# A seventh k-tile pair in Strassen's form, at the second piece, in seven units of a decoder trunk

## The chip, the core and the metric

The kernel runs on one core of one Trainium2 chip. Its time is device microseconds of one execution; the time before is the median of three runs. The profile is of one further execution. Engines: PE is TensorE (PEld its weight loads), DVE VectorE, ACT ScalarE, POOL GpSimd, SP SyncE, which issues most loads.

## The reference

One layer of a decoder trunk, for 256 rows of width 4096, all in fp32:

```python
u = rmsnorm(h, norm_w)
proj = u @ w_in            # a_q a_f a_i a_g  b_q b_k b_v b_g  gate_a gate_b
o_a = rmsnorm(hgrn2_mix(a_q, a_f, a_i, lb), hgrn_norm_w) * silu(a_g)
o_b = rmsnorm(diff_attention(b_q, b_k, b_v, lam, slopes), subln_w) * (1 - lam_init) * silu(b_g)
y = sigmoid(gate_a) * (o_a @ w_branch_a) + sigmoid(gate_b) * (o_b @ w_branch_b)
out = rmsnorm(h + y @ w_out, final_w)
```

`w_in` is 4096 x 24576, the two branch matrices are 2048 x 4096, `w_out` is 4096 x 4096. HGRN2 is a gated recurrence in chunks of 64 rows (16 heads); the differential attention has 8 heads of two maps.

## The kernel before

**Split numbers.** Each fp32 operand is held as two parts of the type fp32r, a high part (a copy of the number) and a low part (the number minus the high part). A product of two 128-deep tiles is three matmuls: high with high, high with low, low with high (L285 to L287, `mm`). For the weights the high part is made by ScalarE (L164, `hi`) and the low part by VectorE (L165, `lo`).

**Units and pieces.** The work is a list of units, each a matrix product that gives 256 rows by 1024 columns. A unit takes its weights in pieces of 128 x 2048 (1 MB): one piece is a pair of k-tiles (256 deep) by 1024 columns. There are 16 mixer units (0 to 7 for the four HGRN groups, two each; 8 to 15 for the four attention groups, two each) and 8 gate units (0 to 7), each of 16 pieces; 8 branch units of 8 pieces; 4 output units of 16 pieces. In a group the first unit gives the channel rows (forget and q, or q and k), the second the gate and the values.

**Plain and Strassen pieces.** A plain piece (kind P) is 8 products of 128 x 128 by 128 x 512, that is 24 matmuls, into the banks 0 to 3 of PSUM. A piece of kind S is done in the Winograd variant of Strassen's form: 7 products, 21 matmuls, into the banks P1, p5, P6, P7, 0, 1 and 2. For it the sums of the left operand (`s_form`, L376) are made once per k-tile pair and kept in the pool `sp` or `sp2` for all units that use them; the sums of the weights are made for each piece by VectorE, in place (L156, L142, L144). The order of the products in an S piece is, by chunk: 0 and 1; p5 and P1; P6; P7 and 2 (L264, `ORDER`). The four banks P1 to P7 are combined when the unit's last S piece is done (L305 to L323). `SPLIT` (L439) says which pieces of mixer units 3 to 15 and of gates 0 and 1 are S: six, from piece 3 on. `SPLIT_G` (nine, piece 1 among them) holds for gates 2 to 6. Mixer units 0 to 2 and gate 7 are plain; while unit 1 runs, u is normalised, and while unit 2 runs, the sums of u are made (`u_sums`, L455). The sums that only `SPLIT_G` needs are made in gate 1 (`more_sums`, L462), into `sp2`.

**Chunks and rings.** The parts of a piece are made in chunks: two of 1024 columns for a plain piece; three of 1024 and one of 512 for an S piece (its third). They go through a ring of six slots for `hi` and six for `lo`, five chunks ahead of use (L146, L171), so a chunk can be made when the one six before it has been used. The last pair of a unit keeps both of its chunks to the unit's end, since its products are done bank by bank. Raw weights have three buffers of 1 MB, filled by SyncE's queue.

**The order of work.** The framework orders each engine's instructions itself, by priority among those that are ready by its own estimate of time; the split of the weights runs under a raised priority (`AHEAD`, L40, L151). So the order in a queue may differ from that of the program.

**What runs beside the units.** The elementwise and small matrix work of the groups stands in a list (`todo`, L217), whose items are TensorE items (transposes, scores, outputs: they borrow one of the four banks P1 to P7 through `spare`, L61, in the order P6, P7, P1, p5) or plain ones. After each piece `step` (L222) takes from its head: a plain item, after which it returns, or up to two TensorE items, these only after the pieces in `OPEN` (L232), when the S products do not use the four banks. For an HGRN group the items run as follows: the first unit's four results are transposed (two after its last piece, two after piece 0 of the second unit; L752, L780), then `s1b`, `s1c`, `s1d`, `s2` (L796 to L826) come one per piece, then the three scores (L828) after pieces 14 and 15, then the two output products (`pv`, L845), one after piece 15 and one after piece 0 of the next unit, then the closing steps (`finish`, L688: root, sigmoid gate L699, scaling L706), and the transposes of the result (L709) after piece 14.

Of the kernel before, what the change touches and what calls it, by code (L numbers as in the profile page):

```python
# [19 lines left out]
S = 256  # L20
# [23 lines left out]
def trunk_kernel(ctx, tc, xT, x, nw, w_mix, w_gate, w_branch, w_out, lbt, hnw, lamv, slw, fw, out):  # L44
# [5 lines left out]
    wraw = ctx.enter_context(tc.tile_pool(name="wraw", bufs=3))  # L50
    whi = ctx.enter_context(tc.tile_pool(name="whi", bufs=6))
    wlo = ctx.enter_context(tc.tile_pool(name="wlo", bufs=6))
    sp = ctx.enter_context(tc.tile_pool(name="sp", bufs=6))
    gp = ctx.enter_context(tc.tile_pool(name="gp", bufs=5))
    psb = ctx.enter_context(tc.tile_pool(name="psb", bufs=1, space=PSUM))
    dram = ctx.enter_context(tc.tile_pool(name="dram", bufs=1, space=DRAM))
# [4 lines left out]
    def spare(shape, name):  # L61

        spare.at += 1
        return psb.tile(shape, F32, name=name, tag=f"b{(6, 7, 4, 5)[spare.at % 4]}")
# [152 lines left out]
    todo = deque()  # L217

    def later(f, pe_=False):
        todo.append((f, pe_))  # L220

    def step(n):  # L222
        for _ in range(2):
            if not todo or (todo[0][1] and n not in OPEN):
                return
            f, pe_ = todo.popleft()
            if f is not None:
                f()
            if not pe_:
                return  # L230

    OPEN = (14, 15, 0, 1, 2)  # L232


    plan = []

    def add(srcs, fn, kinds, post=None):

        for n, s in enumerate(srcs):
            stream.append(s, kinds[n])  # L240
            plan.append((n, fn, post))

    def run(upto):
        for i in range(run.at, upto):
            n, fn, post = plan[i]
            stream.load_to(i + LOAD_AHEAD)
            for c, (hi, lo) in enumerate(stream.take(i)):
                fn(n, c, hi, lo)
            if post:
                post(n)  # L250
            step(n)
        run.at = upto

    run.at = 0
# [14 lines left out]
    def wide_unit(srcs, kinds, pf, sf, bank, final, post=None, tail=1, kt0=0, pre=None):  # L269
# [62 lines left out]
        def fn(n, c, hi, lo):  # L332
# [19 lines left out]
            for blocks in ([[(t, 1 - m)] for t in range(2) for m in range(2)] if tail == 1  # L352
                           else [[(0, 0), (0, 1)], [(1, 0)], [(1, 1)]]):
                for (k, c2), w in held.items():
                    plain(k, c2, *w, blocks)

        add(srcs, fn, kinds, post)

    PLAIN = ["P"] * 16

    def mix(n, s):
        return ["S" if i in s else "P" for i in range(n)]

    def gate_unit(q, kinds, sf, bank, post=None):
        def final(t, n, ps, g):
            if g is None:
                g = gp.tile([P, 512], F32, name="gt", tag="gt")
                act.activation(g, ps, AF.Sigmoid)
            else:
                dve.tensor_tensor(g, ps, g, op=ALU.add)  # L370
                act.activation(g, g, AF.Sigmoid)
            pool.dma_start(g_dram[2 * q + n][t], g)

        wide_unit([w_gate[q, n] for n in range(16)], kinds, u, sf, bank, final, post)

    def s_form(f):  # L376

        s = gp.tile([P, 4, P], F32, name="s", tag="gt")
        a11, a21, a12, a22 = (f[:, k, t * P : (t + 1) * P] for k in range(2) for t in range(2))
        dve.tensor_tensor(s[:, 0], a21, a22, op=ALU.add)  # L380
        dve.tensor_tensor(s[:, 1], s[:, 0], a11, op=ALU.subtract)
        dve.tensor_tensor(s[:, 2], a21, a11, op=ALU.subtract)
        dve.tensor_tensor(s[:, 3], a12, s[:, 1], op=ALU.subtract)
        t = s_pool().tile([P, 4, 2, P], F32R, name="sf", tag="sf")
        act.activation(t[:, :, 0, :], s, AF.Copy)
        dve.tensor_tensor(t[:, :, 1, :], s, f32(t[:, :, 0, :]), op=ALU.subtract)
        return t
# [5 lines left out]
    def joined(n):  # L393

        f = gp.tile([P, 2, S], F32, name="f", tag="gt")
        t, k = u[n // 2], 2 * (n % 2)
        dve.tensor_tensor(f, f32(t[:, k : k + 2, 0, :]), f32(t[:, k : k + 2, 1, :]), op=ALU.add)
        return f
# [37 lines left out]

    SPLIT = (3, 5, 7, 9, 11, 13)  # L439
    SPLIT_G = (1, 3, 5, 6, 7, 9, 11, 13, 14)  # L440
    us = {}
    s_pools = [sp]
# [12 lines left out]
    def u_sums(which):  # L455
        def f(n):
            if n in which:
                us[n] = s_form(joined(n))
        return f


    def more_sums(n):  # L462
        if n == 0:
            s_pools[:] = [sp2]
        if n in SPLIT_G and n not in SPLIT:
            us[n] = s_form(joined(n))
# [27 lines left out]
    def o_end():  # L494
        o_split(14)
        o_split(15)
# [19 lines left out]
    def y_next(n):  # L516
        if n > 0:
            y_split(n - 1)
        y_load(n)

    def branch_unit(q):
        rows, g, merge = {}, {}, []

        def g_load(br):
            for n in range(2):
                for t in range(2):
                    gl = g[t, n] = op.tile([P, 512], F32, name="gl", tag=("fw", "xr")[n], bufs=2)
                    nc.sync.dma_start(gl, g_dram[8 * br + 2 * q + n][t])

        def gated(t, n, ps, c, dst):  # L530
            if c is not None:
                dve.tensor_tensor(c, ps, c, op=ALU.add)  # L532
                ps = c
            dve.tensor_tensor(dst, ps, g[t, n], op=ALU.mult)

        def a_final(t, n, ps, c):
            if n == 1:
                r = sp2.tile([P, 2, 512], F32, name="rows", tag="sf")
                rows[t, 0], rows[t, 1] = r[:, 0], r[:, 1]
            gated(t, n, ps, c, rows[t, n])  # L540

        def b_final(t, n, ps, c):
            gated(t, n, ps, c, g[t, n])
            merge.append((t, n))
            if len(merge) == 4:
                later(add_rows)
                for i in merge:
                    later(lambda i=i: turn(*i), True)

        def add_rows():  # L550
            for i in merge:
                dve.tensor_tensor(rows[i], rows[i], g[i], op=ALU.add)

        def turn(t, n):
            ps = spare([P, 4, P], "ps_y")
            for j in range(4):
                pe.transpose(ps[:, j], rows[t, n][:, j * P : (j + 1) * P], ident)
            yt = gp.tile([P, 4, P], F32, name="yt", tag="gt")
            act.activation(yt, ps, AF.Copy)
            pool.dma_start(y_dram[2 * q + n][:, :, t * P : (t + 1) * P], yt)  # L560

        def post(n):
            if n == 0:
                g_load(0)
                if q == 0:
                    o_end()

        def post_b(n):
            if n == 0:
                g_load(1)  # L570
            if q == 3:
                if n == 0:
                    s_pools[:] = [sp] * 6 + [sp2]
                    s_pool.at = -1
                y_next(n)

        wide_unit([w_branch[0, q, n] for n in range(8)], mix(8, SPLIT_B), oh, os, bank, a_final, post)
        wide_unit([w_branch[1, q, n] for n in range(8)], mix(8, SPLIT_B), oh, os, bank, b_final, post_b, kt0=16)


# [84 lines left out]
    def declare_rest():  # L665
        gate_unit(1, mix(16, SPLIT), us, bank, post=more_sums)
        for q in range(2, 7):
            gate_unit(q, mix(16, SPLIT_G), us, bank)
        gate_unit(7, PLAIN, None, bank, post=o_next)
        for q in range(4):  # L670
            branch_unit(q)
        for q in range(4):
            out_unit(q)


    with tc.tile_pool(name="tmp", bufs=1) as tmp:
# [52 lines left out]

        def mixer_unit(final, pre=None, turned=None):  # L730
            m = next(unit)
            kinds = PLAIN if m < 3 else mix(16, SPLIT)
            post = (None, u_norm, u_sums(SPLIT))[m] if m < 3 else None
            scale = m < 2

            def fin(t, n, ps, tile_):
                dst = final(t, n, tile_)
                if tile_ is not None:
                    dve.tensor_tensor(dst, ps, tile_, op=ALU.add)
                elif scale:  # L740
                    act.activation(dst, ps, AF.Copy, scale=rstd[:, t : t + 1])
                else:
                    act.activation(dst, ps, AF.Copy)
                if turned:
                    later(lambda: turned(t, n, dst), True)

            wide_unit([w_mix[m, n] for n in range(16)], kinds, u, us, bank, fin, post, pre=pre)
# [236 lines left out]
        for g in range(4):  # L984
            attn_group(g)
        gate_unit(0, mix(16, SPLIT), us, bank)
        end_of_mixers = len(plan)
        declare_rest()
        run(end_of_mixers)
        while todo:  # L990
            f, _ = todo.popleft()
# [2 lines left out]

    whi2 = ctx.enter_context(tc.tile_pool(name="whi2", bufs=1))
    wlo2 = ctx.enter_context(tc.tile_pool(name="wlo2", bufs=1))
    sp2 = ctx.enter_context(tc.tile_pool(name="sp2", bufs=3))
    op = ctx.enter_context(tc.tile_pool(name="op", bufs=2))
    stream.ring = [(whi, wlo)] * 6 + [(whi2, wlo2)]
    stream.at = 0  # L1000
    stream.ahead = 5
    run(len(plan))
_OUT = (S, D)

# [47 lines left out]
```

## Time and profile before

| | |
|---|---|
| median of 3 runs | 2777.52 us (2777.48 to 2779.8) |
| the profiled execution | 2780.43 us, span 2778.7 us |
| PE busy | 2756.5 us (99%), 12361 instructions |
| PE weight loads | 2276.1 us (82%) |
| DVE busy | 2333.0 us (84%) |
| ACT busy | 1627.4 us (59%) |
| POOL busy | 73.2 us (3%) |
| read from HBM, written | 571.51 MB, 24.12 MB (214 GB/s over the span) |
| granted clock of TensorE | 0.999 |

In the profile a matmul's busy time is longer than its distance to the next one, since matmuls are pipelined; a unit's speed is better read from the number of its matmuls and its length. The waits list who an engine waited for. In a timeline a row gives start, length, engine, line, instruction, what it writes and reads, the count of merged instructions, and the idle time before it with what ended it.

### The profile page before, as it was taken

How to read it: one execution, taken by the hardware profiler on the slowest of the kernel's cores; microseconds unless marked ns; L12 is line 12 of the kernel's file. 1: busy time of each engine (PE TensorE's matmuls, PEld its weight loads, DVE VectorE, ACT ScalarE, POOL GpSimd, SP SyncE). 2: the span in 40 equal slices, each digit the busy share in tenths (PEclk: the TensorE clock that was granted, in tenths of full speed). 3: DMA queues.
4: the chain of work that ended last, by engine and by line, in shares of the span. 5: the costliest groups of instructions: out<-in, count | busy, mean ns of one | idle time of the engine just before them, and what ended most of it. 6: DMA issues, size and time to landing. Idle time of an engine off the chain costs nothing. (4 is left out here: it accounts for less than half of the span.)

```text
span 2778.7 us, 32845 instructions
## 1 busy us (share of the span) xinstructions
PE 2756.5 (99%) x12361; PEld 2276.1 (82%) x12361; DVE 2333.0 (84%) x2709; ACT 1627.4 (59%) x2017; POOL 73.2 (3%) x124
## 2 busy tenths in 40 slices
PE   9999999999999999999999999999999999999998
PEld 7888888888888888888888888888888888887886
DVE  6784888888888888888888999999867888989987
ACT  7664666656656555565565555565655554555555
POOL 0010000000000000000000000000000000010000
PEclk9999999999999999999999999999999999999999
DMA  9555455555455545555456655555665766666665
GB/s 359 187 175 194 185 183 200 201 214 188 182 190 212 205 177 202 190 212 193 178 199 232 228 210 200 226 203 231 252 244 206 257 225 230 246 227 246 242 253 223
DMA packets 96767, 597.76 MB, mean 215 GB/s; under 512 B 11856, under 2 KB 12128, under 8 KB 31200
## 3 DMA queue, kind: packets, MB, share of 16 engines
q1 hardware_dynamic: 87696, 564.72, 55.6%
q0 software_dynamic: 8336, 29.38, 2.9%
q8 instruction: 96, 1.57, 0.2%
q10 hardware_dynamic: 576, 1.57, 0.1%
q14 instruction: 63, 0.52, 0.1%
HBM read 571.51 MB, written 24.12 MB: 214 GB/s over the span
## 5 line engine op out<-in xcount | busy, mean ns | idle before, releaser
L164 ACT ACTIVATE hi<-w 128x1024 fp32r<-128x1024 f32 (+1 forms) x1378 | 1338.8, 999 | 1028.5 <-PE ps_w L287 584.7
L165 DVE TENSOR_TENSOR lo<-w,hi 128x1024 fp32r<-128x1024 f32 (+1 forms) x1378 | 1547.1, 1150 | 323.6 <-ACT hi L164 311.9
L287 PE MATMUL ps_w<-hi,u 128*128 128x512 f32 x4794 | 1537.4, 391 | 4.1 <-DVE ut L370 3.4
L287 PEld LDWEIGHTS ps_w<-hi,u 128*128 128x128 f32 x4794 | 900.6, 188 | 193.5 <-ACT hi L164 3.8
L287 PE MATMUL ps_w<-lo,u 128*128 128x512 f32 x2397 | 933.8, 390 | 0.0
L287 PEld LDWEIGHTS ps_w<-lo,u 128*128 128x128 f32 x2397 | 450.6, 188 | 92.3 <-DVE lo L165 0.4
L287 PE MATMUL ps_w<-hi,sf 128*128 128x512 f32 x1400 | 490.6, 390 | 0.2
L287 PEld LDWEIGHTS ps_w<-hi,sf 128*128 128x128 f32 x1400 | 262.8, 188 | 55.6 <-ACT hi L164 1.2
L287 PE MATMUL ps_w<-lo,sf 128*128 128x512 f32 x700 | 273.5, 391 | 4.5 <-DVE lo L165 4.3
L287 PE MATMUL ps_w<-hi,oh 128*128 128x512 f32 x864 | 272.7, 390 | 0.0
L287 PE MATMUL ps_w<-hi,y 128*128 128x512 f32 x784 | 250.6, 390 | 0.7 <-DVE ut L532 0.4
L144 DVE TENSOR_TENSOR w<-w 128x1024 f32<-128x1024 f32 x175 | 213.5, 1220 | 1.8
L287 PEld LDWEIGHTS ps_w<-hi,oh 128*128 128x128 f32 x864 | 162.0, 188 | 34.2 <-DVE ut L532 0.9
L287 PEld LDWEIGHTS ps_w<-hi,y 128*128 128x128 f32 x784 | 147.2, 188 | 32.0 <-DVE ut L532 0.8
L287 PE MATMUL ps_w<-lo,oh 128*128 128x512 f32 x432 | 168.5, 390 | 0.0
L287 PEld LDWEIGHTS ps_w<-lo,sf 128*128 128x128 f32 x700 | 131.4, 188 | 35.6 <-DVE lo L165 9.0
L287 PE MATMUL ps_w<-lo,y 128*128 128x512 f32 x392 | 152.6, 389 | 0.0
L156 DVE TENSOR_TENSOR w<-w 128x512 f32<-128x512 f32 x175 | 120.1, 687 | 24.3 <-DMA w<-in_w_mix 10.3
L142 DVE TENSOR_TENSOR w<-w 128x512 f32<-128x512 f32 x175 | 120.4, 688 | 3.3
L287 PEld LDWEIGHTS ps_w<-lo,oh 128*128 128x128 f32 x432 | 81.1, 188 | 16.5
L287 PEld LDWEIGHTS ps_w<-lo,y 128*128 128x128 f32 x392 | 73.6, 188 | 15.1
L721 POOL DMA_DIRECT2D o_dram<-s x8 | 4.4, 550 | 945.8 <-ACT s L720 596.8
(196 smaller groups left out, 1026.9 us busy)
## 6 DMA issues: line engine op xcount, KB each, us to landing
w<-in_w_mix SPq DMA_DIRECT2D x252, 1024.0 KB, 4.8
w<-in_w_gate SPq DMA_DIRECT2D x128, 1024.0 KB, 4.9
w<-in_w_branch SPq DMA_DIRECT2D x64, 1024.0 KB, 4.8
w<-in_w_out SPq DMA_DIRECT2D x64, 1024.0 KB, 4.9
gl<-g_dram SPq DMA_DIRECT2D x32, 256.0 KB, 3.1
g_dram<-ut POOLq DMA_DIRECT2D x28, 256.0 KB, 2.7
o_dram<-s POOLq DMA_DIRECT2D x8, 512.0 KB, 7.0
ol<-o_dram SPq DMA_DIRECT2D x16, 256.0 KB, 3.4
```

What stands on the lines that cost most here:

```text
L142: dve.tensor_tensor(t2, w[:, 0:512], t2, op=ALU.subtract)
L144: dve.tensor_tensor(b, b, t2.unsqueeze(1).to_broadcast([P, 2, 512]), op=ALU.subtract)
L156: dve.tensor_tensor(w[:, 0:512], w[:, 0:512], w[:, 512:1024], op=ALU.add)
L164: act.activation(hi[:, k : k + m], t[:, k : k + m], AF.Copy)
L165: dve.tensor_tensor(lo[:, k : k + m], t[:, k : k + m], f32(hi[:, k : k + m]), op=ALU.subtract)
L287: pe.matmul(ps[b], a, w, start=first, stop=left[b] == 0)
L721: pool.dma_start(o_dram[slot], oT)
```

## The change

Units 3 to 7 and gates 0 and 1 get a seventh S piece, piece 1. `SPLIT` now begins with 1, and units 8 to 15 use it without its first entry. In units whose piece 1 is S, TensorE items may be taken after pieces 14, 15 and 0 only, and up to four items after piece 0 (still ending at a plain item). The sums for piece 1 are made in unit 2 instead of gate 1, and lie in `sp`, which gets a seventh buffer; `sp2` has two instead of three. The sums of the output units' left operand all go to `sp`.

```diff
-    sp = ctx.enter_context(tc.tile_pool(name="sp", bufs=6))
+    sp = ctx.enter_context(tc.tile_pool(name="sp", bufs=7))
...
-    def step(n):
-        for _ in range(2):
-            if not todo or (todo[0][1] and n not in OPEN):
+    def step(n, early):
+        for _ in range(4 if early and n == 0 else 2):
+            if not todo or (todo[0][1] and n not in OPEN[early]):
                 return
...
-    OPEN = (14, 15, 0, 1, 2)
+    OPEN = ((14, 15, 0, 1, 2), (14, 15, 0))
...
-            plan.append((n, fn, post))
+            plan.append((n, fn, post, kinds[1] == "S"))
...
-            step(n)
+            step(n, early)
...
-    SPLIT = (3, 5, 7, 9, 11, 13)
+    SPLIT = (1, 3, 5, 7, 9, 11, 13)
...
-                    s_pools[:] = [sp] * 6 + [sp2]
+                    s_pools[:] = [sp]
...
-            kinds = PLAIN if m < 3 else mix(16, SPLIT)
+            kinds = PLAIN if m < 3 else mix(16, SPLIT[m > 7 :])
...
-    sp2 = ctx.enter_context(tc.tile_pool(name="sp2", bufs=3))
+    sp2 = ctx.enter_context(tc.tile_pool(name="sp2", bufs=2))
```

More of the change, by code (lines that the diff above doesn't have):

```diff
@@ L240, in add @@
             stream.append(s, kinds[n])
-            plan.append((n, fn, post))
+            plan.append((n, fn, post, kinds[1] == "S"))
     def run(upto):
         for i in range(run.at, upto):
-            n, fn, post = plan[i]
+            n, fn, post, early = plan[i]
             stream.load_to(i + LOAD_AHEAD)
```

## The prediction

> **What bounds the kernel now.** I read the page first, for the engines' shares and the groups; then the windows, one per unit; then the waits of TensorE; then timelines around single pieces. From the page:
>
> ```profile
> span 2778.7 us, 32845 instructions
> ## 1 busy us (share of the span) xinstructions
> PE 2756.5 (99%) x12361; PEld 2276.1 (82%) x12361; DVE 2333.0 (84%) x2709; ACT 1627.4 (59%) x2017; POOL 73.2 (3%) x124
> ```
>
> TensorE is busy nearly throughout, but its matmuls overlap, so this alone does not say that it is the bound. The windows below are (in order) unit 2, unit 4, unit 5, a stretch inside unit 5, gate 1, gate 4 and output unit 2. A unit's ends come from counting its matmuls: 24 for a plain piece, 21 for one in Strassen's form. Columns: length, then busy time and count of TensorE, its weight loads, VectorE, ScalarE, GpSimd, then granted clock, DMA share and GB/s.
>
> ```profile
> 189.10:279.60 90.50, 90.50 (x417) 75.36 (x416) 44.53 (x47) 44.71 (x63) 0.56 (x1) 1.00 0.53 184
> 367.10:453.70 86.60, 86.60 (x401) 72.19 (x401) 71.26 (x80) 52.04 (x71) 0.55 (x1) 1.00 0.54 193
> 453.70:541.20 87.50, 87.50 (x409) 73.11 (x408) 75.63 (x82) 57.94 (x70) 1.73 (x2) 1.00 0.55 200
> 460.10:471.10 11.00, 11.00 (x52) 9.10 (x50) 10.10 (x14) 10.87 (x19) 0.00 (x0) 1.00 0.16 48
> 1501.40:1584.50 83.10, 83.10 (x368) 68.59 (x367) 70.80 (x82) 44.65 (x51) 1.07 (x2) 1.00 0.62 227
> 1749.30:1832.20 82.90, 81.79 (x357) 66.78 (x357) 79.46 (x86) 49.51 (x57) 2.14 (x4) 1.00 0.57 217
> 2602.50:2684.70 82.20, 82.20 (x364) 68.10 (x363) 76.14 (x84) 46.81 (x57) 3.23 (x6) 1.00 0.64 237
> ```
>
> Gate 1 issues its own 366 matmuls in 83.10 us: one per 0.227 us. Output unit 2 with seven Strassen pieces runs 363 in 82.20 us, 0.226 each: seven such pieces cost TensorE no wait there, with VectorE busy 76.1 of 82.2 us (93%). Gate 4 with nine has VectorE at 79.5 of 82.9 us (96%) and needs 82.9 us where 357 x 0.227 = 81.0 would do. So the time is TensorE's issue rate, until VectorE's share passes some 93%; what ends the wait then is the low part of the split, as TensorE's waits in gates 2 to 6 show (total us, times, longest):
>
> ```profile
> PE ps_w L287 <- DVE lo L165: 2.4, 3, 1.0
> ```
>
> **What is removed.** Seven units change a plain piece 1 into Strassen's form: units 3 to 7, gate 0 and gate 1. Three matmuls less in each, 21 in all, at 0.227 us: 4.77 us, if TensorE stays the bound. This is the ceiling of the gain by this term.
>
> **What VectorE and ScalarE get for it.** Prices, from the groups of VectorE in output unit 2, shapes kept apart:
>
> ```profile
> L165 DVE TENSOR_TENSOR lo<-w,hi 128x1024 fp32r<-128x1024 f32 x39 | 46.4, 1220 | 4.3 <-ACT hi L164 3.9
> L144 DVE TENSOR_TENSOR w<-w 128x1024 f32<-128x1024 f32 x7 | 8.6, 1224 | 0.1
> L142 DVE TENSOR_TENSOR w<-w 128x512 f32<-128x512 f32 x7 | 4.8, 687 | 0.1
> L156 DVE TENSOR_TENSOR w<-w 128x512 f32<-128x512 f32 x7 | 4.8, 686 | 1.1 <-DMA w<-in_w_out 1.1
> L165 DVE TENSOR_TENSOR lo<-w,hi 128x512 fp32r<-128x512 f32 x7 | 4.8, 684 | 0.0
> ```
>
> A plain piece has two low parts (2.44 us). A Strassen piece has three and a half-size one (4.34) and the three sums (2.60). The difference is 4.5 us in five more instructions. Neighbours overlap by about 0.09 us (below, two of 1.22 make 2.35), so it takes about 4.05 us of the engine. ScalarE gets one full and one half-size high part, 1.7 us by the full one's 1.0 (half of a row below that holds two) and the half-size one's 0.61.
>
> On average that fits. Unit 5 goes to 79.7 of 86.8 us (92%), unit 4 to 75.3 of 85.9 (88%), gate 1, which loses one sum-form, to about 73 of 82.4; all are below output unit 2's 93%. Nothing comes in unit 2 but the sum-form for piece 1: it stands in a unit in which VectorE is busy 44.5 of 90.5 us and ScalarE 44.7, so I cost it at 0; if that cover were gone it would cost its 2.5 us of VectorE.
>
> **Where it does not fit: units 3, 5 and 7.** These run the HGRN arithmetic in pieces 1 to 5. VectorE in unit 5, and the matmul that takes the low part of piece 5's last chunk (start, us, engine, line, work, count, idle before):
>
> ```profile
> 459.65 1.22 DVE L165 TENSOR_TENSOR lo<-w,hi 128x1024 fp32r<-128x1024 f32 x1 [3.56 <-ACT hi L164]
> 472.13 1.22 DVE L818 TENSOR_TENSOR z<-z,s 128x1024 f32<-128x1024 f32 x1 [0.51 <-ACT s L813]
> 481.42 2.36 DVE L165 TENSOR_TENSOR lo<-w,hi 128x1024 fp32r<-128x1024 f32 x2
> 484.90 0.39 PE L287 MATMUL ps_w<-lo,sf 128*128 128x512 f32 x1
> 458.56 2.00 ACT L164 ACTIVATE hi<-w 128x1024 fp32r<-128x1024 f32 x2
> ```
>
> The low part is there at 481.42 + 1.22 = 482.64, and is taken at 484.90: 2.26 us to spare, the least of this unit. In unit 3 the same place has less:
>
> ```profile
> 308.33 2.35 DVE L165 TENSOR_TENSOR lo<-w,hi 128x1024 fp32r<-128x1024 f32 x2
> 310.86 0.39 PE L287 MATMUL ps_w<-lo,sf 128*128 128x512 f32 x1
> ```
>
> 308.33 + 1.22 = 309.55 against 310.86: 1.31 us. After the change TensorE arrives 3 x 0.227 = 0.68 us earlier. VectorE's 4.05 us mostly fall before 459.65: the sums into the end of the previous unit, the last two chunks of piece 1 into the stretch up to the 3.56 us gap. They cannot start sooner, as the ring of six chunks hands them the slots that the previous unit's last pair holds to its end. This pushes piece 2's two chunks back by their slots, and with them piece 3's. I put VectorE's lateness at piece 4 at about 1.1 us (the one low part too many, after the gap is filled). ScalarE matters more: two high parts (the 2.00 us row) move into 460.1 to 471.1, where it is busy 10.87 of 11.0 us; then the exponentials, and L818 behind them, are late by up to 2.0 us. So the spare is 2.26 - 0.68 - (1.1 to 2.0) = +0.5 to -0.4 in units 5 and 7, and 1.31 - 0.68 - (1.1 to 2.0) = -0.5 to -1.4 in unit 3. I take 0.9 us for unit 3 and 0.2 each for units 5 and 7: 1.3 us. Ends: 0, and 8.4 if none of the 4.05 us finds idle time (4.05 + 0.68 - 2.26 = 2.5, twice, and 4.05 + 0.68 - 1.31 = 3.4).
>
> **The banks.** Piece 1 now needs the four banks that transposes, scores and outputs borrow. In units 4 and 6 the second output product stands right before piece 1. By the order of borrowing it sits on P1 in unit 4 and on P7 in unit 6. Its copy is late, since ScalarE does a table load and a sigmoid first (unit 4; the row of TensorE is the first of piece 1):
>
> ```profile
> 374.42 0.48 PE L287 MATMUL ps_w<-hi,u 128*128 128x512 f32 x1
> 375.86 1.28 ACT L699 ACT_TABLE_LOAD   x1
> 377.15 1.06 ACT L699 ACTIVATE s<-g 128x1024 f32<-128x1024 f32 x1
> 378.12 0.61 ACT L164 ACTIVATE hi<-w 128x512 fp32r<-128x512 f32 x1
> 378.64 0.58 ACT L862 ACTIVATE z<-ps_o 128x512 f32<-128x512 f32 x1
> ```
>
> The bank is free at 379.22, 4.8 us into piece 1. P1's turn comes after 9 matmuls (2.0 us), P7's after 15 (3.4): waits of 2.8 and 1.4 us if TensorE stands still. What would stand behind P1's product are P6's, P7's and bank 2's, and piece 2. But the order of TensorE is made by readiness, and this case shows a late bank being passed by. In unit 9, piece 3, the second half's transposes borrow P6's bank:
>
> ```profile
> 825.54 0.27 PE L942 MATMUL ps_at<-ident,s 128*128 128x128 f32 x1
> 825.57 0.48 PE L287 MATMUL ps_w<-hi,sf 128*128 128x512 f32 x1
> 828.06 0.27 PE L944 MATMUL ps_at<-ident,s 128*128 128x128 f32 x1
> 828.91 0.50 PE L287 MATMUL ps_w<-hi,sf 128*128 128x512 f32 x1
> ```
>
> The last Strassen product of piece 3 starts at 828.91, behind the transposes and behind plain matmuls of piece 4, without a gap. So I take 0.2 us for both units, nearer this row; ends 0 and 4.2.
>
> **The steps.** In units 3, 5 and 7 the step after piece 0 takes two transposes and one plain item instead of two transposes, so the HGRN items come one piece earlier in program order. Four TensorE items never stand there. ScalarE starts them as soon as the transposes are copied already; I cost it at 0. Later items (scores at pieces 14 and 15) are not moved. No DMA is added.
>
> **Gate 1** loses the sum-form of piece 1 and gains the Strassen piece. VectorE there today:
>
> ```profile
> 1506.57 0.29 DVE L380 TENSOR_TENSOR s<-f 128x128 f32<-128x128 f32 x1 [3.06 <-DMA g_dram<-ut]
> 1518.12 0.69 DVE L156 TENSOR_TENSOR w<-w 128x512 f32<-128x512 f32 x1 [3.17 <-DMA w<-in_w_gate]
> 1520.07 1.22 DVE L165 TENSOR_TENSOR lo<-w,hi 128x1024 fp32r<-128x1024 f32 x1
> 1521.44 0.40 PE L287 MATMUL ps_w<-lo,sf 128*128 128x512 f32 x1
> ```
>
> The low part is there at 1521.29 and taken at 1521.44: 0.15 us to spare, after 6.2 us of idle behind two DMAs. Without the sum-form for piece 1 the first wait can go, or piece 6's sum-form can take its place and its wait. Ends: 0, and 4.05 - 2.0 (the sum-form, less overlap) + 0.68 - 0.15 = 2.6 us. I take 0.5, near the lower end, as there is idle of both kinds to fill. Gate 0 (only late gating work at its start) I cost at 0.
>
> **Sum.** -4.77 + 1.3 + 0.2 + 0.5 = -2.8 us. The profiled execution took 2780.43 us, 1.7 more than its span and 2.9 more than the median 2777.52; the sum is a difference, so it goes onto the median: 2774.7 us. About 0.2% (5.6 us) is what a measurement of this kernel can tell from no change, so even the full 4.77 us would count as the same.
>
> **Rivals.**
> 1. Everything is hidden: 2777.52 - 4.77 = 2772.8. It belongs to the forecast's own range, 2772.5 to 2777.5; together 0.70. For it: units 3 to 7 show no wait of TensorE, and output unit 2 carries seven pieces. Against: the spare of 1.31 us.
> 2. The banks make TensorE stand in units 4 and 6: -2.8 + 4.0 = +1.2, 2778.7, "same". For it: the copy is 4.8 us late. Against: unit 9. Chance 0.13.
> 3. Slower: the HGRN crunch decides. Place: pieces 1 to 5 of units 3, 5, 7, and piece 3 of gate 1. ScalarE, full from 460.1 to 471.1, delays the exponentials, VectorE waits at L818 with the splits behind it, and none of the added 4.05 us is hidden. Price 8.4 + 2.6 - 4.77 = +6.2, 2783.7. It decides from 10.4 us of lost time on (4.77 + 5.6). Against: 3.56 us idle before 459.65 and 92% on average. Chance 0.09.
> 4. Faster by more than 0.2%: the order of VectorE's queue downstream comes out better as well. Gates 2 to 6 lose some 1.9 us each against the issue rate (82.9 - 81.0); a third of these 9.5 regained on top of the forecast gives -2.8 - 3.2 = -6.0, 2771.5. Nothing in the change aims there, only the sequence shifts. Chance 0.08.
>
> The Trainium skill ("Perfetto Trace Analysis", Identifying the Most-Contended Engine) says that matmul busy time is no good measure of headroom and that TensorE should be judged by its weight loads instead, the other engines by occupancy. By this rule VectorE (84%) stands above the weight loads (82%), and the change adds work to the most contended engine, which is rival 3's side; were all of it on the path, 7 x 4.05 - 4.77 would be some 24 us more, an estimate. The row of output unit 2 disagrees: VectorE at 93% and not a wait.
>
> **Chances and range.** Faster 0.08 (rival 4), same 0.70 + 0.13 = 0.83, slower 0.09 (rival 3). The range goes from rival 4's time to somewhat above rival 2's, 2771.5 to 2780.5; it leaves out rival 3 and half of rival 4.
>
> **What would show it.** Right: units 3 to 7 and gates 0 and 1 each shorter by up to 0.68 us; 21 matmuls fewer on L287; no idle of TensorE in units 4 and 6; a wait of under 1.5 us on a low part about piece 5 of unit 3. Rival 2 would show as a wait on L862, rival 3 as waits on L165 of 2 us and more in units 3, 5 and 7. The forecast is wrong if gates 2 to 6 or the output units change by more than they lose now.

## The result and the profile after

The changed kernel takes **2780.99 us** (median of 20 runs, 2777.33 to 2786.16), the kernel before on the same chip 2777.47 us (20 runs, 2774.88 to 2783.17): ratio 1.0013, 95% interval 1.0007 to 1.0019. So it is 3.5 us slower where 2.8 us faster was forecast, and 0.5 us above the range. The profiled execution spans 2780.3 us, 1.6 more than the one before; single executions of either kernel lie up to 9 us apart, so the profiles are compared stretch by stretch, and the medians decide on the whole.

The span and the engines, from the page of the changed kernel:

```profile
span 2780.3 us, 32844 instructions
PE 2754.5 (99%) x12340; PEld 2274.2 (82%) x12340; DVE 2355.8 (85%) x2744; ACT 1637.0 (59%) x2031; POOL 78.4 (3%) x124
```

TensorE has 21 instructions fewer, as said, and 2 us less busy time, in a span that is longer: it now stands still for longer. Lines lie one later than before (L287 is L288, L841 L842, L854 L855); L164 and L165 are where they were. The longest waits of TensorE after (total us, times, longest):

```profile
PE ps_w L288 <- DVE lo L165: 7.2, 9, 2.3
PE ps_o L855 <- POOL s L842: 4.6, 1, 4.6
```

The second row is one single wait for GpSimd, the engine that is busy for 3% of the span. Before, the same wait was there and small:

```profile
PE ps_o L854 <- POOL s L841: 0.3, 1, 0.3
```

Where the time went, by stretch (us, ends found by counting matmuls; the last columns are experiments told below):

| stretch | before | after | sums alone | mask | late sums | late sums, loads moved |
|---|---|---|---|---|---|---|
| units 1 and 2 | 182.76 | 189.49 | 189.70 | 182.20 | 182.20 | 182.22 |
| units 3 to 7 | 435.57 | 432.65 | 435.55 | 432.68 | 432.70 | 432.63 |
| gate 0 | 84.09 | 83.44 | 84.09 | 83.41 | 83.42 | 83.44 |
| gate 1 | 83.06 | 84.90 | 82.96 | 82.84 | 83.19 | 82.28 |
| gates 2 to 7 | 501.19 | 497.96 | 500.09 | 496.81 | 497.77 | 496.99 |

The other units change by 0.2 us together. (The branch and output units alone take 690.5 to 698.6 us over the nine profiles of this document, which is why the whole spans of single profiles say little here.) The seven units that were edited come out much as forecast. The loss is in units 1 and 2, of which nothing but the place of one sum-form was changed: 6.7 us. The windows of these two units (columns as in the prediction), first before:

```profile
96.90:279.70 182.80, 182.53 (x844) 152.11 (x842) 129.41 (x169) 105.95 (x142) 7.60 (x3) 1.00 0.53 184
```

and after, units 1 and 2 together and then the end of unit 1 and the start of unit 2 in pieces:

```profile
97.00:286.50 189.50, 184.94 (x843) 154.14 (x842) 133.39 (x178) 106.49 (x144) 11.84 (x3) 0.98 0.49 175
180.00:186.00 6.00, 6.00 (x35) 5.21 (x35) 6.00 (x16) 5.04 (x9) 4.29 (x1) 1.00 0.55 198
186.00:192.40 6.40, 1.91 (x13) 1.56 (x11) 5.92 (x14) 3.96 (x6) 6.40 (x2) 0.88 0.19 69
192.40:194.40 2.00, 1.94 (x9) 1.94 (x10) 0.00 (x0) 0.00 (x0) 0.60 (x2) 0.50 0.96 393
196.40:197.40 1.00, 1.00 (x4) 0.73 (x3) 0.77 (x2) 0.33 (x1) 0.00 (x0) 0.50 0.00 0
198.40:199.40 1.00, 1.00 (x6) 0.80 (x5) 0.00 (x0) 0.55 (x1) 0.00 (x0) 1.00 0.00 0
```

TensorE works for 1.91 of the 6.40 us from 186.0, and afterwards its granted clock is 0.50 and comes back to 1.00 by 198.4. The wait itself is 4.56 us:

```profile
192.47 2.08 PE L855 MATMUL ps_o<-v,s 128*128 128x128 f32 x8 [4.56 <-POOL s L842]
```

It is the first output product of the first HGRN group. It takes the scores, which GpSimd masks in place (L841 before, the select). The select runs twice there, once for each block of scores. Duration in ns (minimum, median, maximum) and starts, before:

```profile
L841 POOL TENSOR_SCALAR_AFFINE_SELECT s<-s x2: 679/3540/6402, 181.7 to 188.0; 128x512 f32<-128x512 f32 x2
```

and after:

```profile
L842 POOL TENSOR_SCALAR_AFFINE_SELECT s<-s x2: 630/5663/10696, 181.7 to 192.4; 128x512 f32<-128x512 f32 x2
```

The same instruction on the same shape takes 0.63 us the second time and 6.40 or 10.70 us the first time. Both start at 181.7; they end with something on VectorE. VectorE's timeline before (start, length, engine, line, work):

```profile
187.09 0.28 DVE L382 TENSOR_TENSOR s<-f 128x128 f32<-128x128 f32 x1
187.29 0.28 DVE L381 TENSOR_TENSOR s<-s,f 128x128 f32<-128x128 f32 x1
187.60 0.60 DVE L383 TENSOR_TENSOR s<-f,s 128x128 f32<-128x128 f32 x1
188.13 1.65 DVE L165 TENSOR_TENSOR lo<-w,hi 128x1024 fp32r<-128x1024 f32 x1
```

and after:

```profile
186.74 0.29 DVE L384 TENSOR_TENSOR s<-f,s 128x128 f32<-128x128 f32 x1
...
187.35 0.29 DVE L382 TENSOR_TENSOR s<-s,f 128x128 f32<-128x128 f32 x1
187.55 0.69 DVE L398 TENSOR_TENSOR f<-u 128x512 f32<-128x512 f32 x1
188.15 1.22 DVE L165 TENSOR_TENSOR lo<-w,hi 128x1024 fp32r<-128x1024 f32 x1
189.29 0.29 DVE L384 TENSOR_TENSOR s<-f,s 128x128 f32<-128x128 f32 x1
...
190.62 0.69 DVE L392 TENSOR_TENSOR u<-f,u 128x512 fp32r<-128x512 f32 x1
191.23 0.29 DVE L381 TENSOR_TENSOR s<-f 128x128 f32<-128x128 f32 x1
191.43 0.29 DVE L383 TENSOR_TENSOR s<-f 128x128 f32<-128x128 f32 x1
191.63 0.29 DVE L382 TENSOR_TENSOR s<-s,f 128x128 f32<-128x128 f32 x1
```

These are instructions with two inputs, each of which starts before the modelled end of the one ahead (187.09 + 0.28 = 187.37 against 187.29). Before, there is a first gap of 0.03 us, from 187.57 to 187.60. The first select ends 0.5 us after it, at 181.66 + 6.40 = 188.06, and TensorE waits 0.3 us. After, the stretch without a gap lasts to 191.92; the first select ends 0.5 us later, at 192.41. L381 to L384 are sum-forms: work of unit 2, which the order puts into unit 1's end. With the seventh one the stretch lasts 4.3 us longer. That is more than the work of one sum-form, some 2 us (2.0 in the prediction): what counts is the gap. Before, L383 at 187.60 takes what L381 directly ahead of it has just made, and by the trace it starts when L381 is done; hence the 0.03 us. After, the same two steps (L382 at 187.35, L384 at 189.29) have other work between them, no gap arises, and two low parts join the stretch.

### The profile page after: what moved, and what is told of

It reads as the page before. It is cut to its first block, busy times and chain, and to the rows that moved or that the text cites. A ratio compares the mean times of both kernels' runs of the same rounds, so it can differ in the third digit from the quotient of the medians.

```text
span 2780.3 us, 32844 instructions
## 1 busy us (share of the span) xinstructions
PE 2754.5 (99%) x12340; PEld 2274.2 (82%) x12340; DVE 2355.8 (85%) x2744; ACT 1637.0 (59%) x2031; POOL 78.4 (3%) x124
## 5 line engine op out<-in xcount | busy, mean ns | idle before, releaser
L164 ACT ACTIVATE hi<-w 128x1024 fp32r<-128x1024 f32 (+1 forms) x1392 | 1348.7, 997 | 1023.5 <-PE ps_w L288 538.2
L165 DVE TENSOR_TENSOR lo<-w,hi 128x1024 fp32r<-128x1024 f32 (+1 forms) x1392 | 1558.5, 1147 | 298.7 <-ACT hi L164 287.5
L288 PE MATMUL ps_w<-hi,u 128*128 128x512 f32 x4724 | 1519.6, 391 | 1.5 <-ACT hi L164 0.8
L288 PEld LDWEIGHTS ps_w<-hi,u 128*128 128x128 f32 x4724 | 888.5, 188 | 188.8 <-DVE ut L371 2.5
L288 PE MATMUL ps_w<-lo,u 128*128 128x512 f32 x2362 | 921.0, 390 | 0.2 <-DVE lo L165 0.2
L288 PEld LDWEIGHTS ps_w<-lo,u 128*128 128x128 f32 x2362 | 444.5, 188 | 91.4 <-DVE lo L165 1.0
L288 PE MATMUL ps_w<-hi,sf 128*128 128x512 f32 x1456 | 510.3, 390 | 0.0
L288 PEld LDWEIGHTS ps_w<-hi,sf 128*128 128x128 f32 x1456 | 273.3, 188 | 57.4 <-ACT q L949 0.6
L288 PE MATMUL ps_w<-lo,sf 128*128 128x512 f32 x728 | 284.7, 391 | 7.1 <-DVE lo L165 7.0
L288 PE MATMUL ps_w<-hi,oh 128*128 128x512 f32 x864 | 272.7, 390 | 0.0
L288 PE MATMUL ps_w<-hi,y 128*128 128x512 f32 x784 | 250.0, 389 | 0.0
L144 DVE TENSOR_TENSOR w<-w 128x1024 f32<-128x1024 f32 x182 | 222.7, 1224 | 2.0
L288 PEld LDWEIGHTS ps_w<-hi,oh 128*128 128x128 f32 x864 | 162.0, 188 | 34.2 <-DVE ut L533 0.9
L288 PEld LDWEIGHTS ps_w<-hi,y 128*128 128x128 f32 x784 | 147.2, 188 | 30.6
L288 PEld LDWEIGHTS ps_w<-lo,sf 128*128 128x128 f32 x728 | 136.7, 188 | 40.1 <-DVE lo L165 12.5
L288 PE MATMUL ps_w<-lo,oh 128*128 128x512 f32 x432 | 168.4, 390 | 0.0
L156 DVE TENSOR_TENSOR w<-w 128x512 f32<-128x512 f32 x182 | 124.9, 686 | 34.1 <-DMA w<-in_w_mix 14.4
L288 PE MATMUL ps_w<-lo,y 128*128 128x512 f32 x392 | 152.6, 389 | 0.0
L142 DVE TENSOR_TENSOR w<-w 128x512 f32<-128x512 f32 x182 | 126.0, 692 | 2.9
L288 PEld LDWEIGHTS ps_w<-lo,oh 128*128 128x128 f32 x432 | 81.1, 188 | 16.5
L288 PEld LDWEIGHTS ps_w<-lo,y 128*128 128x128 f32 x392 | 73.6, 188 | 15.2
```

What stands on the lines that cost most here:

```text
L142: dve.tensor_tensor(t2, w[:, 0:512], t2, op=ALU.subtract)
L144: dve.tensor_tensor(b, b, t2.unsqueeze(1).to_broadcast([P, 2, 512]), op=ALU.subtract)
L156: dve.tensor_tensor(w[:, 0:512], w[:, 0:512], w[:, 512:1024], op=ALU.add)
L164: act.activation(hi[:, k : k + m], t[:, k : k + m], AF.Copy)
L165: dve.tensor_tensor(lo[:, k : k + m], t[:, k : k + m], f32(hi[:, k : k + m]), op=ALU.subtract)
L288: pe.matmul(ps[b], a, w, start=first, stop=left[b] == 0)
```

## The experiments

The theory after the traces: GpSimd's select cannot run while VectorE's two-input instructions follow one another without a gap, and TensorE hangs on the select. Rivals for units 1 and 2: the select is slow because it is the first of its form on GpSimd; the loss comes with the Strassen pieces, not the sum; the price is VectorE's time for the sum. Apart from that, gate 1's wait (84.90 us, below) could be the forecast's lack of VectorE or a late load.

**Sums alone.** The kernel before, with the seventh sum-form made in unit 2, kept in `sp` and not made in gate 1; the Strassen pieces stay six.

```diff
-    sp = ctx.enter_context(tc.tile_pool(name="sp", bufs=6))
+    sp = ctx.enter_context(tc.tile_pool(name="sp", bufs=7))
...
-        if n in SPLIT_G and n not in SPLIT:
+        if n in SPLIT_G and n not in SPLIT and n != 1:
...
-                    s_pools[:] = [sp] * 6 + [sp2]
+                    s_pools[:] = [sp]
...
-            post = (None, u_norm, u_sums(SPLIT))[m] if m < 3 else None
+            post = (None, u_norm, u_sums((1,) + SPLIT))[m] if m < 3 else None
...
-    sp2 = ctx.enter_context(tc.tile_pool(name="sp2", bufs=3))
+    sp2 = ctx.enter_context(tc.tile_pool(name="sp2", bufs=2))
```

> The kernel before, with one part of the change alone: the sum-form for piece 1 is made in unit 2 instead of gate 1 (sp seven, sp2 two buffers). SPLIT keeps six pieces, so no matmul is saved. Theory A (the select on GpSimd cannot start while VectorE runs two-input instructions back to back, and the seventh sum-form, taken early, lengthens that stretch at the end of unit 1): the first select of unit 1 takes about 10.7 us instead of 6.4, TensorE waits some 4.6 us for it, units 1 and 2 are together 6 to 7 us longer, and the whole 4 to 7 us slower than before (gate 1 may give a little back). Theory B (the select's length is chance or the cost of its first use, and the time went somewhere else): the select is 6 to 7 us again and the time is within 2 us of before.

Measured: 2782.63 us against 2778.1, ratio 1.0016 (1.0007 to 1.0025). The selects, and the wait of TensorE:

```profile
L841 POOL TENSOR_SCALAR_AFFINE_SELECT s<-s x2: 632/5664/10697, 181.7 to 192.4; 128x512 f32<-128x512 f32 x2
PE ps_o L854 <- POOL s L841: 4.6, 1, 4.6
```

With no Strassen piece added the whole loss is there, the select as long to within a nanosecond (10697 against 10696). The sum-form's place costs it, not the seven pieces.

**The mask without GpSimd, in the changed kernel and in the one before.** A table of ones and zeros is made once at the start. VectorE multiplies the scores by it as it copies them out of PSUM, in place of ScalarE's copy and GpSimd's select.

```diff
...
-                    act.activation(sc, ps, AF.Copy)
                     if tb < 2:
-                        pool.affine_select(sc, sc, pattern=[[0, HPG], [1, P]], base=0,
-                                           channel_multiplier=-1, compare_op=ALU.is_ge, fill=0.0)
+                        dve.tensor_tensor(sc, ps, tri.unsqueeze(1).to_broadcast([P, HPG, P]), op=ALU.mult)
+                    else:
+                        act.activation(sc, ps, AF.Copy)
```

> The changed kernel, with the causal cut of the scores done by VectorE (a product with a table of ones and zeros, in place of ScalarE's copy and GpSimd's select). Theory A: TensorE's wait of 4.6 us at the end of unit 1 and the slow clock behind it in unit 2 are gone, units 1 and 2 are back at 182.5 to 183.5 us in all, and the kernel is 5 to 7 us faster than the changed one, 2 to 4 us faster than before. Theory B, first use: the same, so this run tells the place of the loss, not its mechanism. Theory C (the loss of the whole lies in gate 1 and the downstream gates, and the select varies from run to run): within 2 us of the changed kernel.

> The kernel before with the same cut on VectorE: the base for the run with the cut in the changed kernel. Theory A: before waited only 0.3 us for the select, so within 1.5 us of before; the changed kernel with the cut on VectorE is then faster than this one by the matmuls saved in units 3 to 7 and gate 0 (3.6 us) less what gate 1 loses (1.8): 1 to 4 us.

Measured: the changed kernel with it 2774.6 us against 2778.1, ratio 0.9985 (0.9976 to 0.9994); the kernel before with it 2778.51, ratio 1.0001 (0.9992 to 1.001). The windows of units 1 and 2, and of gates 2 to 7, of the changed kernel with the mask:

```profile
96.90:279.10 182.20, 182.20 (x842) 152.04 (x841) 134.31 (x180) 105.03 (x141) 0.56 (x1) 1.00 0.51 182
1580.35:2077.15 496.80, 494.68 (x2170) 406.23 (x2169) 452.15 (x498) 294.59 (x337) 13.81 (x26) 1.00 0.61 227
```

Units 1 and 2 lose 7.3 us, to 182.20, with TensorE busy throughout, though VectorE does as much as in the changed kernel (134.31 us against 133.39). So the price was not VectorE's time. The rest of the change, with the select out of the way in both, is 2774.6 - 2778.51 = -3.9 us: a gain of the forecast's size was there, hidden behind one wait. It is not the forecast's alone: by the profiles of these two kernels gates 2 to 7, which the forecast left alone, give 2.6 us of it (499.42 to 496.81).

**An early select.** The changed kernel, with one more select of the same form on a scratch tile at the start.

```diff
+    trial = gp.tile([P, HPG, P], F32, name="trial", tag="gt")
+    pool.memset(trial, 0.0)
+    pool.affine_select(trial, trial, pattern=[[0, HPG], [1, P]], base=0,
+                       channel_multiplier=-1, compare_op=ALU.is_ge, fill=0.0)
```

> The changed kernel with one more select of the same shape on a scratch tile at the start, when VectorE is idle. Theory A: the first select of unit 1 still takes 9 to 11 us and the time is that of the changed kernel within 1.5 us. Theory B (first use): that select takes about 0.7 us, and the kernel gets 5 to 7 us faster.

Measured: 2780.88 us against 2778.1, ratio 1.0009 (0.9999 to 1.0018). The selects of the first group:

```profile
L846 POOL TENSOR_SCALAR_AFFINE_SELECT s<-s x2: 632/5664/10696, 181.9 to 192.6; 128x512 f32<-128x512 f32 x2
```

Still 10.70 us, so a first use is not the reason.

**Late sums.** The changed kernel with all seven sum-forms kept and only their time changed: the first instruction of each reads a one-column tile that holds 1.0 and that VectorE writes in the closing steps of the first HGRN group (`finish`), so no sum-form can be finished ahead of that (one step of the first, which does not read that tile, still runs at 170.2).

```diff
-        dve.tensor_tensor(s[:, 0], a21, a22, op=ALU.add)
+        dve.scalar_tensor_tensor(s[:, 0], a21, one, a22, op0=ALU.mult, op1=ALU.add)
...
+            if slot == 0:
+                dve.tensor_scalar(late, ss[:, 7:8], 0.0, 1.0, op0=ALU.mult, op1=ALU.add)
```

> The changed kernel, select left on GpSimd; the seven sum-forms of unit 2 now read a factor of 1.0 that is made from the first group's last square sums, so none of them can be taken in unit 1: VectorE's stretch at the end of unit 1 ends earlier. Theory A (the select cannot start while VectorE's two-input instructions follow each other without a gap, and the early sum-forms made that stretch): the first select falls below 6 us, TensorE does not wait for it, units 1 and 2 take 182 to 183 us, the time is 5 to 7 us below the changed kernel and 2 to 5 us below before. If the select itself is slow at this place whatever VectorE does, it stays at 10 us and the time at the changed kernel's.

Measured: 2773.45 us against 2777.02, ratio 0.999 (0.9981 to 0.9998). The selects, and the window of units 1 and 2:

```profile
L848 POOL TENSOR_SCALAR_AFFINE_SELECT s<-s x2: 632/919/1206, 181.8 to 183.0; 128x512 f32<-128x512 f32 x2
```

```profile
97.40:279.60 182.20, 182.20 (x842) 152.04 (x841) 133.48 (x179) 106.68 (x144) 2.35 (x3) 1.00 0.51 182
```

GpSimd's instruction is untouched, VectorE's total is the same (133.48 us), and the first select takes 1.21 us instead of 10.70. What differs is that VectorE has gaps at that time:

```profile
181.28 1.23 DVE L165 TENSOR_TENSOR lo<-w,hi 128x1024 fp32r<-128x1024 f32 x1 [0.26 <-ACT hi L164]
187.55 1.23 DVE L165 TENSOR_TENSOR lo<-w,hi 128x1024 fp32r<-128x1024 f32 x1 [5.04 <-ACT hi L164]
```

The select starts at 181.80, beside the first of these. That one is done at 181.28 + 1.23 = 182.51, VectorE then stands idle, and the select ends at 183.00, again 0.5 us later. That settles what holds the select: the work on VectorE beside it, and its place in time.

**Gate 1 plain.** The changed kernel with the mask, and gate 1's piece 1 plain again.

```diff
-        gate_unit(1, mix(16, SPLIT), us, bank, post=more_sums)
+        gate_unit(1, mix(16, SPLIT[1:]), us, bank, post=more_sums)
```

> The changed kernel with the causal cut on VectorE, and gate 1 without the seventh Strassen piece (piece 1 plain again, its sum-form still made in unit 2). Theory D (the 3 us that gates 2 to 7 are shorter in all kernels with the change come from the order that follows gate 1's Strassen piece): gates 2 to 7 go back to 499 to 501 us, and the kernel is 2 to 4 us slower than the one with the cut on VectorE alone. Theory E (they come from the earlier units, or the buffers): gates 2 to 7 stay at 497 to 498 us, gate 1 takes 83.1, and the time is within 1 us of it.

Measured: 2774.68 us against 2777.02, ratio 0.9992 (0.9984 to 1.0001). Gates 2 to 7 take 499.61 us in its profile. In the profiles of the five kernels in which gate 1's piece 1 is in Strassen's form they take 496.8 to 498.0, in the four in which it is plain 499.4 to 501.2. So the 3 us that gates 2 to 7 lost come with gate 1's piece in these profiles, though nothing in these gates was edited. The whole time does not show this clearly: 2.3 us under the kernel before here, 3.5 us with the piece, so 1.2 us where 2 to 4 were expected, in two comparisons whose intervals overlap.

**Late sums, and the gate loads off SyncE's queue.** The reason for this run lies in gate 1 of the changed kernel. The issues on SyncE's queue, VectorE and TensorE there:

```profile
1507.79 8.50 SPq L529 DMA_DIRECT2D gl<-g_dram  x3
1516.40 0.36 SPq L130 DMA_DIRECT2D w<-in_w_gate  x1
1524.56 0.69 DVE L156 TENSOR_TENSOR w<-w 128x512 f32<-128x512 f32 x1 [6.64 <-DMA w<-in_w_gate]
1526.44 0.50 PE L288 MATMUL ps_w<-lo,sf 128*128 128x512 f32 x1 [2.33 <-DVE lo L165]
```

SyncE stands for 8.5 us on three loads of gate values (`gl`, for the branch units, put far ahead by the order; 7.3 us of it are a wait for the store of such values, `g_dram`), and the weights behind them are issued only at 1516.40. They land 8.1 us later; VectorE is idle for 6.64 us and TensorE waits 2.33 us at piece 3. In this run the loads of the gate values are issued by GpSimd:

```diff
-                    nc.sync.dma_start(gl, g_dram[8 * br + 2 * q + n][t])
+                    pool.dma_start(gl, g_dram[8 * br + 2 * q + n][t])
```

> As the run with the late sum-forms, and the loads of the gates for the branch units go out on GpSimd's queue instead of SyncE's, so that SyncE's loads of weights in gate 1 do not stand behind loads that wait for the gates' stores. Theory F (the wait of 2.3 us in piece 3 of gate 1 in the changed kernel's profile is a late weight load behind them): the weights for piece 5 of gate 1 are issued as soon as their buffer is free, gate 1 takes 82.4 us or little more, and the time is 0 to 2.5 us below the run with the late sum-forms alone. If the load is late for the traffic alone, gate 1 stays between 82.3 and 84.9.

Measured: **2771.11 us** against 2777.02, ratio 0.998 (0.9971 to 0.9989). Gate 1 there, and the issues on SyncE's queue:

```profile
1494.60:1576.90 82.30, 82.30 (x364) 68.15 (x363) 73.99 (x82) 48.73 (x55) 4.85 (x9) 1.00 0.62 233
1498.50 15.56 SPq L130 DMA_DIRECT2D w<-in_w_gate  x4
```

Only weights stand in the queue, TensorE does not wait, and gate 1 has 0.78 us less than before the change (82.28 against 83.06), a little more than its three matmuls. This kernel is 5.9 us faster than the one before, and so faster than the changed one. From late sums alone the step is 2773.45 to 2771.11; by the intervals (0.9981 to 0.9998, 0.9971 to 0.9989) it is likely, not certain, and gate 1 shows only 0.9 us of it (83.19 to 82.28).

Nor is SyncE's stand by itself the cause of the 2.33 us. In the profiles with the mask, with the early select and with late sums, SyncE stands on these loads in gate 1 for 7.39, 7.28 and 7.46 us, nearly as long; the same weights land 17.7, 17.0 and 18.1 us after gate 1's start, and TensorE's waits for low parts there are 0.2, 0 and 0.6 us. In the changed kernel they land at 19.9 us: issued 1.0 to 1.2 us later than in these three, and 8.1 us on their way instead of 6.5 to 7.4. With the loads moved they go out at 8.5 us, when their buffer comes free, instead of 11.7, and land at 13.5. So the stand took the reserve, and a slower transfer on top of it made the wait; why the transfer was slower is not shown.

## Why the prediction was wrong

**The step that failed** is the last of the paragraph on VectorE and ScalarE: "Nothing comes in unit 2 but the sum-form for piece 1 ... so I cost it at 0; if that cover were gone it would cost its 2.5 us of VectorE." Both halves fell. The sum-forms did not run in unit 2, whose VectorE is half idle: the order had moved them forward (27 of the 28 additions and subtractions of the seven start before 192 us) into the end of unit 1, where VectorE is busy without a gap (6.00 of 6.00 us from 180.0). And what they cost there is not VectorE's 2.5 us, but 4.3 more of GpSimd's select (6.40 to 10.70), which becomes 4.56 - 0.3 = 4.3 us of TensorE's wait. To this comes the clock: from 192.4 to about 197.6 it is 0.50, which loses some 2.6 us by half of that time. 4.3 + 2.6 = 6.9, against 6.7 measured for both units. With 0 in the sum replaced by 6.7, -2.8 becomes +3.9; measured were +3.5. That these are so near is luck, since other terms were off as well: units 3 to 7 and gate 0 by -1.0 us, gate 1 by +2.0, gates 2 to 7 by -3.2 (below).

The profile of before had the warning: a select of 6402 ns beside one of 679, and a wait of 0.3 us for GpSimd. The prediction took TensorE's waits by their size and GpSimd by its 3%, and did not ask where in the order the sums of unit 2 stood.

By the Trainium skill ("SBUF — State Buffer", Who interferes with whom), a VectorE instruction with two inputs in SBUF and a GpSimd instruction that reads SBUF exclude each other, and the one that comes second waits until the other is through. The trace agrees that the select waits beside such work: 10.70 us in the gapless stretch, 1.21 with the sums elsewhere. That it waited out 25 instructions in a row, and not one, is what this trace shows. The lock itself is in no row; it is inferred from the select's ends, 0.5 us behind VectorE's first gap in both kernels. No run put instructions with one input there, so that two inputs are needed is not shown here.

**The ceiling, 21 x 0.227 = 4.77 us:** right. Units 3 to 7 and gate 0 give 2.92 + 0.65 = 3.57 us of their 18 x 0.227 = 4.09.

**HGRN crunch, 1.3 us:** too much. Units 3 and 5 gain 0.71 us each, the full three matmuls, and TensorE does not wait in them. VectorE's share in unit 5 is what was worked out (79.7 of 86.8):

```profile
459.30:546.10 86.80, 86.80 (x406) 72.57 (x405) 79.46 (x88) 59.03 (x72) 2.17 (x2) 1.00 0.52 194
```

The least spare in unit 3 is:

```profile
313.98 3.49 DVE L165 TENSOR_TENSOR lo<-w,hi 128x1024 fp32r<-128x1024 f32 x3
316.97 0.39 PE L288 MATMUL ps_w<-lo,sf 128*128 128x512 f32 x1
```

The low part is there at 313.98 + 1.21 = 315.19 and taken at 316.97: 1.78 us to spare, where -0.5 to -1.4 was forecast, so the chain from ScalarE's two extra high parts to L818 did not carry their 2.0 us. Counted from the unit's start (279.68 before, 286.50 after), this low part is not late at all: it is there after 28.69 us instead of 29.87. Why it comes earlier is not shown. (The 1.7 us of high parts in the prediction are 1.6 by its own two numbers, 1.0 + 0.61; no term hangs on the difference.) Rival 3 did not come about, though its sign did.

**Banks, 0.2 us:** about right. In unit 4 the late copy (L863) and the first matmul of piece 1:

```profile
380.53 0.48 PE L288 MATMUL ps_w<-hi,u 128*128 128x512 f32 x1
386.12 0.58 ACT L863 ACTIVATE z<-ps_o 128x512 f32<-128x512 f32 x1
```

The bank comes free 6.2 us into piece 1, even later than the 4.8 that was worked out, and TensorE has no gap there: it passes the late bank by, as in unit 9. Units 4 and 6 gain 0.50 us instead of 0.68. Unit 7, with no such bank, gains 0.50 too, so the missing 0.18 is not shown to be the bank's. Rival 2 is out.

**Gate 1, 0.5 us:** the second term that was mis-sized, inside its ends. It came out at 84.90 - (83.06 - 0.68) = 2.5 us, against the end of 2.6. Its place was right (piece 3, a low part late behind DMAs), with a wait of 2.33 us. But the chain starts one step further back than the prediction had it, at SyncE's queue, and its size hangs on how long the weights take to land: with nearly the same stand the term is 0.8 us with late sums, 0.5 with the mask and -0.1 with the early select, and without the stand -0.1 (82.28).

**Gates 2 to 7,** which the forecast left alone, take 3.2 us less. That is about rival 4's place (gates 2 to 6) and its price (3.2 us); the agreement of the size is luck, as the price was a guess of one third. A gain there is seen in all five kernels with gate 1's Strassen piece. Why the order downstream comes out better is not settled.

The stretches make 6.7 - 3.6 + 1.8 - 3.2 - 0.2 = +1.5, against +1.6 of the spans. The medians have +3.5: the profiled executions lie 2.9 us (before) and 1.0 us (after, 2782.0) above their medians, and one profile each cannot say where that sits.

## What to carry to other kernels

When work is added "in a unit with room", look up where the order really puts it: an edit that adds independent work may land one unit earlier, beside a chain that it does not belong to. In the trace of before, look for an instruction that now and then takes ten times its usual time: it waits for something that the profile does not name, and anything that lengthens that something goes straight to the one who waits for it. An engine at 3% can hold the one at 99%; and a small mask or copy on the way to TensorE is better put on an engine that does not compete for it, or the competing work made to come later.

## What was not expected of the hardware

- A GpSimd select of 128 x 512 that takes 0.63 us by itself took 6.40 and 10.70 us beside VectorE instructions with two inputs that left no gap; it did not get in between two of them, over 25 instructions, and ended 0.5 us after the first gap, which before the change was 0.03 us long. Elsewhere a visible gap was not needed: in unit 3 of the changed kernel a select that started at 366.97 ended at 368.11, 0.5 us after a low part (L165) that ended at 367.61, though VectorE's next instruction (L142) had started at 367.53; that one took 1.12 us instead of 0.69. What decides who gets in is not shown. The other way it was seen as well: VectorE's instructions at the time when the select finished took 0.60 us (L383) and 1.65 us (L165) instead of 0.28 and 1.22.
- A stand of TensorE of 4.56 us cost about 2.6 us more by the clock: 0.50 for 5.2 us after it, then 1.00 again. The 0.3 us stand before the change left the clock at 1.00. By the Trainium skill ("TensorE: Matmul & The Clock Gate", What's actually happening) an idle time of some 3.4 us halves the clock, and it comes back after a busy time of as much, counted in windows that do not start with the work; the trace agrees with the halving, and its 5.2 us lies between one such window and two.
- Loads in one queue stand behind one that waits: 8.5 us on SyncE in gate 1, for gate values that were needed only in the branch units. The weights behind them went out 3.2 us later after gate 1's start than with these loads moved (11.7 against 8.5 us).
